# A two-layer hybrid decoder trunk: the first gate/up group computed as seven products like the rest, softmax divisors gathered, all root-mean-square sums as high/low pairs

## The chip, the cores and the metric

The kernel runs on one core of one Trainium2 chip. The metric is the device time of one execution in microseconds (us); the figure for a kernel is the median of its runs. A core has five engines with a queue of instructions each: TensorE (PE, matrix products, with a queue of its own for loading weights, PEld), VectorE (DVE), ScalarE (ACT), GpSimd (POOL) and SyncE (SP), which issues most of the transfers. An engine waits for another by semaphores.

## The reference

The input is 1024 tokens of 1024 numbers, the depth is two layers, and everything is float32. A layer normalises, projects, runs four token mixers side by side, projects back, and then runs a gated feed-forward network (FFN) of inner width 2816:

```python
for l in range(DEPTH):
    h = rmsnorm(x, attn_norm[l])
    proj = h @ w_in[l]
    (c_q, c_kv, k_r, g_b, g_c, u_conv, u_pool,
     q_sw, k_sw, v_sw) = jnp.split(proj, pts, axis=-1)
    y_a = mla_attention(c_q, c_kv, k_r, ...)      # causal softmax, 4 heads
    y_b = short_gated_conv(g_b, g_c, u_conv, conv_w[l])
    y_c = multiscale_pool(u_pool, pool_w[l], pool_scale[l])
    y_d = swa_sink_attention(q_sw, k_sw, v_sw, ...)   # window 128, a sink logit per head
    gf = jnp.stack([y_a, y_b, y_c, y_d], axis=2).astype(jnp.float32)
    gf = gf * lax.rsqrt(jnp.mean(gf * gf, axis=-1, keepdims=True) + RMS_EPS)
    mixed = gf.reshape(b, s, D_MIX) * mix_norm[l]
    x = x + mixed @ w_o[l]
    h2 = rmsnorm(x, ffn_norm[l])
    gate, up = jnp.split(h2 @ w_gate_up[l], 2, axis=-1)
    x = x + (jax.nn.silu(gate) * up) @ w_down[l]
return rmsnorm(x, final_norm)
```

## The kernel before

**Products.** Activations lie transposed: 128 channels on the partitions, tokens along the row, in two halves of 512 tokens (t = 0 and 1; `HALVES = (1, 0)`, so half 1 goes first at the end of the mixers). A float32 operand of a large product is split into a high and a low part in a reduced format (fp32r): ACT casts the high part, DVE subtracts it from the original (`split`, L368 and L371; with a gain column L373 and L374). `mm3` (L348) then makes three matmuls for each term of a product: high by high, high by low, low by high.

**Gate and up.** The FFN's 2816 gate and 2816 up columns are taken in 22 groups f of 128 gate and 128 up columns. A group over both token halves is a 2 x 2 block product (even and odd channel blocks by two halves), and a Strassen-like scheme makes it from seven products instead of eight. A product is 4 channel pairs by three matmuls, so 12 matmuls of 128 x 128 by 128 x 512. Its operands on the activation side are `hb[B11]`, `hb[B21]` (half 1 alone), `hb[B22]` (half 0, odd blocks) and the sums N1, N2, T3, T4 of both halves, which `combine(j)` (L1229) makes for pair j: two scalings on ACT, five operations on DVE, and four splits. On the weight side it needs three sums of weight blocks, which POOL makes for most groups (`GateUp.sums`).

**The first groups of a layer.** Group 0 is done plainly (`plain(u)`, L1509): four products for each half, with B11 and B21 for half 1, and B12 and B22 for half 0. No sums stand ahead of it. Groups 1 and 2 are "early": their weight sums are made in DRAM during the mixers by accumulating transfers from POOL's queue (`gu_made`, L322, six transfers a group, each held back by `paced` until a matmul of the current projection), and their steps `start`, `n2`, `n1`, `t3`, `b22`, `t4` are written out by hand around `plain` and `combine`. Group 3 and the later ones run in a loop with their sums on POOL.

**Entry of the FFN.** `out_last(t, ma)` (L1259) adds the last part of the output projection for half t (eight products of six matmuls), and for each block d DVE adds it to the residual (L1274), splits the block by the norm's gain (L374), and adds its square to the sum (L420). So half 1 gives B11 and B21; half 0 gives B12 and B22; `combine(j)` needs both.

**Roots.** The root mean square of each token is a sum over partitions, made by a matmul with a matrix of ones (`SumSq.rnorm`). If the sum's object is a pair (`SumSq(n, True)`), the sum is split into high and low and takes two fp32r matmuls (L428); else it takes one float32 matmul (L431). ACT then makes ln, exp and a square, DVE two more operations (L440, L443).

**Softmax.** In the windowed attention `swa_unit(g, i)` does one key/value group and one block of 128 queries for two heads: scores, maximum, exp with its sum, the sink's exp, addition, reciprocal (L721), scaling of the probabilities (L723), transposes and the product with the values. In the latent attention `scores(h, t, q)` does four query blocks; for each it adds the sums of its two key chunks (t = 1 alone, L1102), takes the reciprocal (L1103) and scales (L1107 on ACT, L1109 on DVE). `mix_values` of one step is called after `scores` of the next.

**Order.** A planner in the kernel (class `Order`) takes the traced instructions, gives each a cost by its kind, lists them engine by engine by due times, tries changes, and fixes the order on every engine, the PSUM banks and the places in SBUF. So a change of the program moves instructions everywhere.

Of the kernel before, what the change touches and what calls it, by code (L numbers as in the profile page):

```python
# [20 lines left out]
P = 128  # L21
# [22 lines left out]
NSP = 3  # L44
NG = NFF // 2
# [81 lines left out]
def trunk_kernel(ctx: ExitStack, tc: tile.TileContext, ins, out, given=None, ends=None):  # L127
# [13 lines left out]
    def rd(ap):  # L141
# [19 lines left out]
        {f: dpool.tile([P, 4 * HT], F32, name=f"gd{l}_{f}") for f in (1, 2)} for l in range(L)  # L161
# [296 lines left out]
    ss = SumSq(D)  # L458
# [59 lines left out]
    for l in range(L):  # L518
# [155 lines left out]
        def swa_unit(g, i):  # L674
# [17 lines left out]
            nm, rs = small(2), small(2)  # L692
# [23 lines left out]
            es = small(2)  # L716
            sk = par[:, l * PC_N + PC_SINK + 2 * g : l * PC_N + PC_SINK + 2 * g + 2]
            dve.tensor_tensor(out=es, in0=nm, in1=sk, op=ALU.add)
            act.activation(es, es, AF.Exp)
            dve.tensor_tensor(out=rs, in0=rs, in1=es, op=ALU.add)  # L720
            dve.reciprocal(rs, rs)  # L721
            for h in range(2):
# [47 lines left out]
        units = deque((g, i) for g in range(2) for i in range(NK))  # L770

        def swa_some(n):
            for _ in range(n):
                if units and qs[2 * units[0][0]][1] is not None:
                    g, i = units.popleft()
                    swa_unit(g, i)
                    if i == NK - 1:
# [7 lines left out]
        def group_scale(g):  # L785

            sg = SumSq(2 * P, g in ("b", "bcd")[l])
# [127 lines left out]
        sq_q = SumSq(2 * P, l > 0)  # L915
# [131 lines left out]
        def scores(h, t, q):  # L1047
# [3 lines left out]
            diag = ((own[0], 0), (own[1], 0), (own[0], P), (own[2], 0))  # L1051
            for b in range(4):
# [9 lines left out]
                rs = small(2)  # L1062
# [38 lines left out]
                if nch == 2:  # L1101
                    dve.tensor_tensor(out=rs[:, 0:1], in0=rs[:, 0:1], in1=rs[:, 1:2], op=ALU.add)  # L1102
                dve.reciprocal(rs[:, 0:1], rs[:, 0:1])  # L1103
                for c in range(nch):
                    a = chunks[c]
                    if c < t and b % 2:
                        act.activation(a, a, AF.Copy, scale=rs[:, 0:1])  # L1107
                        continue
                    dve.tensor_scalar(  # L1109
                        out=a, in0=a, scalar1=rs[:, 0:1], scalar2=None, op0=ALU.mult  # L1110
                    )
                pr.append(chunks)
# [146 lines left out]
        def out_last(t, ma):  # L1259
# [4 lines left out]
            for d in range(NK):  # L1264
# [11 lines left out]
                hb[c][d // 2] = half_split(a, pcol(l, PC_FFN + d))  # L1276
# [11 lines left out]
        class GateUp:  # L1288
# [20 lines left out]

            def split_plain(self):  # L1310
                self.s1, self.s2 = pair_split(self.raw[0]), pair_split(self.raw[1])
                for i in self.raw:
                    F.free_pair(i)
# [34 lines left out]
            def start(self):  # L1348
# [7 lines left out]
                mul_to(self.gate, self.gate, r2[0])  # L1356

            def n2(self):
# [3 lines left out]
                self.own.append(F.half())  # L1362
                self.gate1 = F.ap(self.own[1])
# [16 lines left out]
            def b22(self):  # L1380
                onto(self.pc, tuple(R.ap(i) for i in self.s4), hb[B22])
                for i in self.s4:
                    R.free(i)
# [1016 lines left out]
```

## Time and profile before

| what | us |
|---|---|
| median of three runs | 2031.27 (2031.17 to 2031.62) |
| the profiled execution, its own time | 2031.74 |
| its span from the first to the last instruction | 2030.0 |
| busy in the span: PE / DVE / ACT / POOL | 2018.6 / 1531.2 / 1022.6 / 567.5 |

The two layers lie one after the other: mixers of the first layer to about 360 us, its FFN to about 1015 us, then the second layer. "Busy" of PE is by the profile's modelled ends of matmuls, which overlap; how often a matmul starts says more. Views named below: the page (engine busy times and the chain that ended last), the waits (who waited for whom), the windows (busy time of each engine in a stretch, with the number of instructions in brackets), the timeline (start, length, line, operation) and the groups of instructions by line.

### The profile page before, as it was taken

Reading aid. Unit: us, or ns where it says so; the run is one execution under the profiler, and the core shown is the slowest. Engines: PE = TensorE matmul, PEld = TensorE weight load, DVE = VectorE, ACT = ScalarE, POOL = GpSimd, SP = SyncE. Lnnn points to the kernel's source line nnn. Section 1 sums busy time; section 2 is a strip of 40 time slices with the busy share of each in tenths; the row PEclk is TensorE's granted clock in tenths of the full one; section 3 lists DMA queues with packets and bytes.
Section 4 is the critical chain, followed back from the end, with each engine's and each line's share of the span. In section 5 each row is a group of like instructions: output and inputs, shape, how many; then the busy total and the mean of one; then the engine's idle time right before and its main releaser. Section 6 shows DMA issues by size and latency. Waiting matters only on the chain.

```text
span 2030.0 us, 26831 instructions
## 1 busy us (share of the span) xinstructions
PE 2018.6 (99%) x9418; PEld 1676.7 (83%) x9418; DVE 1531.2 (75%) x2442; ACT 1022.6 (50%) x1778; POOL 567.5 (28%) x428
## 2 busy tenths in 40 slices
PE   9999999999999999999999999999999999999998
PEld 7888888888888888888888888888888888888887
DVE  8779989997666678776646998799976766785554
ACT  7447657843333335555633676677333333354343
POOL 0100000057776772000001000000587677710000
PEclk9999999999999999999999999999999999999999
DMA  5431132336445547998835224332554554487552
GB/s 207 109 63 55 64 108 81 136 131 205 169 164 201 175 163 266 354 371 283 296 100 133 63 91 133 105 126 93 175 168 169 199 172 169 162 301 259 190 178 84
DMA packets 154232, 338.57 MB, mean 167 GB/s; under 512 B 14960, under 2 KB 62192, under 8 KB 154096
## 3 DMA queue, kind: packets, MB, share of 16 engines
q1 hardware_dynamic: 149616, 325.31, 46.6%
q0 software_dynamic: 4480, 11.54, 3.2%
q8 instruction: 74, 1.21, 0.2%
q14 instruction: 62, 0.51, 0.1%
HBM read 241.36 MB, written 105.91 MB: 171 GB/s over the span
## 4 chain that ended last, share of the span: by engine, by line
PE 96%; DVE 0%; DMA 0%; ACT 0%; issue 0%; DVEq 0%; ACTq 0%
PE ps_mm L348 37%; PE ps_s L348 30%; PE ps_t L348 12%; PE ps_pv L348 8%; PE ps_pv L1137 2%; PE ps_t L1125 1%; PE ps_s L1071 1%; PE ps_s L1072 1%; PE ps_s L1073 1%; PE ps_s L685 1%; PE ps_s L943 1%; PE ps_pv L746 1%; PE ps_t L734 1%; PE ps_t L428 0%; DMA xp<-u 0%; PE ps_t L431 0%
## 5 line engine op out<-in xcount | busy, mean ns | idle before, releaser
L348 PE MATMUL ps_mm<-u,u 128*128 128x512 f32 (+1 forms) x3378 | 833.2, 390 | 0.5 <-ACT u L368 0.3
L348 PEld LDWEIGHTS ps_mm<-u,u 128*128 128x128 f32 x3378 | 614.6, 188 | 122.7 <-issue 2.6
L371 DVE TENSOR_TENSOR u<-u,u 128x1024 fp32r<-128x1024 f32 (+3 forms) x453 | 511.3, 1148 | 194.1 <-ACT u L368 176.5
L348 PE MATMUL ps_s<-u,u 128*128 128x512 f32 x2670 | 634.0, 389 | 0.0
L348 PEld LDWEIGHTS ps_s<-u,u 128*128 128x128 f32 x2670 | 501.0, 188 | 104.9 <-issue 0.5
L368 ACT CAST u<-u 128x1024 fp32r<-128x1024 f32 (+3 forms) x453 | 385.2, 868 | 382.9 <-DMA u<-ad 73.9
L348 PE MATMUL ps_t<-u,u 128*128 128x512 f32 (+1 forms) x1124 | 254.4, 377 | 0.0
L348 PEld LDWEIGHTS ps_t<-u,u 128*128 128x128 f32 x1124 | 202.7, 188 | 39.3 <-issue 0.5
L1548 POOL TENSOR_TENSOR tm<-tm,u 128x512 f32<-128x512 f32 x80 | 139.5, 1744 | 341.6 <-ACT tm L1546 337.1
L348 PE MATMUL ps_pv<-u,u 128*128 128x512 f32 x744 | 177.5, 389 | 0.0
L348 PEld LDWEIGHTS ps_pv<-u,u 128*128 128x128 f32 x744 | 139.5, 188 | 29.1 <-ACT u L1364 0.2
L322 POOL DMA_DIRECT2D gd<-in_w_gu x24 | 21.6, 898 | 415.0 <-PE ps_t L348 281.4
L1134 POOL MEMSET u<- 128x128 f32 x32 | 6.1, 217 | 428.7 <-PE ps_mm L348 193.5
L1546 ACT ACTIVATE tm<-tm 128x512 f32<-128x512 f32 x80 | 50.6, 632 | 135.8 <-DVE tm L449 135.7
L368 ACT CAST u<-ps_t 128x512 fp32r<-128x512 f32 (+3 forms) x132 | 65.8, 504 | 54.1 <-PE ps_t L1125 27.0
L371 DVE TENSOR_TENSOR u<-ps_t,u 128x512 fp32r<-128x512 f32 (+3 forms) x132 | 75.7, 582 | 18.9 <-ACT u L368 17.2
L1414 ACT COPY tm<-ps_s 128x512 f32<-128x512 f32 x61 | 35.8, 587 | 101.7 <-PE ps_s L348 101.6
L1626 POOL TENSOR_TENSOR u<-u,u 128x352 f32<-128x352 f32 x64 | 81.4, 1272 | 1.4
L412 ACT ACTIVATE tm<-u 128x512 f32<-128x512 f32 (+1 forms) x91 | 53.9, 600 | 49.2 <-DVE u L1817 41.2
L373 ACT ACTIVATE u<-u,par 128x512 fp32r<-128x512 f32 x99 | 69.4, 715 | 17.8 <-DVE u L1274 7.6
L1626 POOL TENSOR_TENSOR u<-u 128x352 f32<-128x352 f32 x64 | 75.4, 1180 | 3.0 <-DMA u<-in_w_dn 2.8
L374 DVE SCALAR_TENSOR_TENSOR u<-u,par,u 128x512 fp32r<-128x512 f32 x99 | 72.5, 745 | 4.4 <-ACT u L373 4.1
(206 smaller groups left out, 2316.3 us busy)
## 6 DMA issues: line engine op xcount, KB each, us to landing
u<-in_w_gu SPq DMA_DIRECT2D x84, 512.0 KB, 4.1
ad<-u SPq DMA_DIRECT2D x154, 256.0 KB, 3.2
u<-ad SPq DMA_DIRECT2D x70, 512.0 KB, 5.9
u<-in_w_dn SPq DMA_DIRECT2D x64, 352.0 KB, 3.4
qd<-u SPq DMA_DIRECT2D x64, 352.0 KB, 2.5
u<-in_w_in SPq DMA_DIRECT2D x43, 512.0 KB, 5.8
u<-qd SPq DMA_DIRECT2D x32, 512.0 KB, 5.4
u<-in_w_dn SPq DMA_DIRECT2D x24, 512.0 KB, 5.4
```

The costliest lines, as they stand in the source:

```text
L322: paced(pool.dma_start(d, a, **more))
L348: last_mm = pe.matmul(o, w, r, start=start and k == 0 and i == 0, stop=stop and k == n - 1 and i == 2, skip_group_check=again,)
L368: a = act.copy(hi, f)
L371: dve.tensor_tensor(out=lo, in0=f, in1=rd(hi), op=ALU.subtract)
L373: a = act.activation(hi, f, AF.Copy, scale=gain)
L374: dve.scalar_tensor_tensor(out=lo, in0=f, scalar=gain, in1=rd(hi), op0=ALU.mult, op1=ALU.subtract)
L412: act.activation(q, f, AF.Square)
L1137: pe.matmul(py[:, c0:], v_of(j, h), R.ap(s)[:, c0:], start=j == 0 and n == 0, stop=j == nj - 1 and n == 1,)
L1414: act.copy(o, p)
L1546: last_silu = act.activation(g, g, AF.Silu)
L1548: pool.tensor_tensor(out=g, in0=g, in1=r, op=ALU.mult)
L1626: pool.tensor_tensor(out=o, in0=a, in1=b, op=ALU.add)
```

## The change

Four things in words, and the parts of the diff:

1. Group 0 becomes an early group like 1 and 2 (`EARLY = (0, 1, 2)`); `plain`, `plain_gates`, `plain_acts`, `split_plain` and B12 go. Its weight sums are made in DRAM too: six more accumulating transfers in each layer.
2. The hand-written order of the early groups is another: `start` of all three, then `split4` and `b22` of each beside `combine(2)` and `combine(3)`, then `n2` of all, then `n1`, `t3`, `t4` group by group.
3. `swa_pair` takes two query blocks together, and `scores` gathers the sums of four blocks, so additions, reciprocals and the sink's exp are done once for two or four blocks on wider tiles.
4. All `SumSq` objects that take whole halves are pairs: the first norm of the kernel, the group norms c and d and the query norm of layer 0 (two roots each, eight in all).

```diff
+EARLY = (0, 1, 2)
...
-        {f: dpool.tile([P, 4 * HT], F32, name=f"gd{l}_{f}") for f in (1, 2)} for l in range(L)
+        {f: dpool.tile([P, 4 * HT], F32, name=f"gd{l}_{f}") for f in EARLY} for l in range(L)
...
-    ss = SumSq(D)
+    ss = SumSq(D, True)
...
-            sg = SumSq(2 * P, g in ("b", "bcd")[l])
+            sg = SumSq(2 * P, True)
...
-        sq_q = SumSq(2 * P, l > 0)
+        sq_q = SumSq(2 * P, True)
...
+        def swa_pair(g, i):
+
+            nm, rs, es = small(4), small(4), small(4)
+            ps_ = [swa_scores(g, i + n, nm[:, 2 * n :], rs[:, 2 * n :]) for n in range(2)]
...
             act.activation(es, es, AF.Exp)
             dve.tensor_tensor(out=rs, in0=rs, in1=es, op=ALU.add)
             dve.reciprocal(rs, rs)
+            for n in range(2):
+                swa_values(g, i + n, ps_[n], rs[:, 2 * n :])
...
-                if nch == 2:
-                    dve.tensor_tensor(out=rs[:, 0:1], in0=rs[:, 0:1], in1=rs[:, 1:2], op=ALU.add)
-                dve.reciprocal(rs[:, 0:1], rs[:, 0:1])
...
+            both = sums8.rearrange("p (b c) -> p b c", c=2)
+            inv = small(4)
+            if t:
+                dve.tensor_tensor(out=inv, in0=both[:, :, 0], in1=both[:, :, 1], op=ALU.add)
+                dve.reciprocal(inv, inv)
+            else:
+                dve.reciprocal(inv, both[:, :, 0])
+            for b, chunks in enumerate(pr):
+                for c, a in enumerate(chunks):
...
-                hb[c][d // 2] = half_split(a, pcol(l, PC_FFN + d))
+                if c != B12:
+                    hb[c][d // 2] = half_split(a, pcol(l, PC_FFN + d))
...
                 dve.tensor_tensor(out=self.gate, in0=pd, in1=k1, op=ALU.add)
-                mul_to(self.gate, self.gate, r2[0])
+
+            def b22(self):
+                p = ps("ac")
+                product(p, tuple(R.ap(i) for i in self.s4), hb[B22])
...
+                self.gate1 = F.ap(self.own[1])
+                act.copy(self.gate1, p)
 
             def n2(self):
                 onto(self.pa, blocks(self.s2, 1), hb[N2])
...
+                dve.tensor_tensor(out=self.gate1, in0=self.pa, in1=self.gate1, op=ALU.add)
+                mul_to(self.gate, self.gate, r2[0])
                 silu(self.gate, r2[0])
...
-        plain(0)
-        r2.append(F.ap(ss2.rnorm(HALVES[0], tag="pv")))
-        plain_gates()
-        combine(0)
+        r2.append(F.ap(ss2.rnorm(HALVES[0], tag="t")))
         for w in early:
             w.split2()
         early[0].start()
+        r2.append(F.ap(ss2.rnorm(HALVES[1], tag="t")))
+        combine(0)
+        early[1].start()
         combine(1)
-        r2.append(F.ap(ss2.rnorm(HALVES[1], tag="t")))
-        plain_acts()
-        plain(1)
-        early[1].start()
-        combine(2)
...
+        early[2].start()
+        for j, w in zip((2, 3, None), early):
+            if j:
+                combine(j)
+            w.split4()
+            w.b22()
         for w in early:
             w.n2()
...
```

What the planner makes of it, at two places.

On PE in the mixers of layer 0, the root of the pool mixer's norm. `ps_t` is the root's bank, `ones_r` the matrix of ones, the other rows are a projection. Before:

```order
L348 MATMUL ps_mm_1541<-u24_247,u36_1309 128x512 x2
L348 MATMUL ps_mm_1541<-u24_247,u22_1310 128x512
L348 MATMUL ps_mm_1566<-u27_299,u36_1309 128x512 x2
L431 MATMUL ps_t_1415<-u16_1410,ones_r_99 128x512
L348 MATMUL ps_mm_1566<-u27_299,u22_1310 128x512
L348 MATMUL ps_mm_1566<-u29_310,u36_1309 128x512 x2
```

Now:

```order
L349 MATMUL ps_mm_1514<-u21_222,u22_1286 128x512 x2
L349 MATMUL ps_mm_1514<-u21_222,u38_1287 128x512
L349 MATMUL ps_mm_1514<-u23_237,u22_1286 128x512 x2
L429 MATMUL ps_t_1388<-u4_1385,ones_r_101 128x512 x2
L349 MATMUL ps_mm_1514<-u23_237,u38_1287 128x512
L349 MATMUL ps_mm_1514<-u24_249,u22_1286 128x512 x2
```

One float32 matmul has become two fp32r matmuls. Over the program eight go and sixteen come.

On PE at the entry of the FFN of layer 0, where the first matmuls with N2 stand (N2 of pair 0 is `u47_2205` and `u15_2217` as operand of `ps_s_4157` before, `u15_2184` and `u2_2196` as operand of `ps_s_4008`, `ps_s_4066` and `ps_pv_4114` now). Before:

```order
L348 MATMUL ps_s_4220<-u24_4059,u7_3918 128x512 x2
L348 MATMUL ps_s_4220<-u24_4059,u13_3919 128x512
L348 MATMUL ps_s_4157<-u47_2205,u20_4149 128x512
L348 MATMUL ps_s_4157<-u15_2217,u20_4149 128x512
L348 MATMUL ps_s_4157<-u47_2205,u0_4150 128x512
L348 MATMUL ps_t_4219<-u47_2205,u7_3918 128x512
L348 MATMUL ps_t_4219<-u15_2217,u7_3918 128x512
L348 MATMUL ps_t_4219<-u47_2205,u13_3919 128x512
L348 MATMUL ps_t_4219<-u16_3984,u7_3918 128x512 x2
```

Now:

```order
L349 MATMUL ps_t_4115<-u1_3806,u31_4004 128x512 x2
L349 MATMUL ps_s_4008<-u15_2184,u42_3996 128x512
L349 MATMUL ps_s_4008<-u2_2196,u42_3996 128x512
L349 MATMUL ps_s_4008<-u15_2184,u44_3997 128x512
L349 MATMUL ps_s_4066<-u15_2184,u13_4000 128x512
L349 MATMUL ps_t_4115<-u1_3806,u23_4005 128x512
L349 MATMUL ps_t_4115<-u17_3836,u31_4004 128x512 x2
L349 MATMUL ps_t_4115<-u17_3836,u23_4005 128x512
L349 MATMUL ps_s_4066<-u2_2196,u13_4000 128x512
L349 MATMUL ps_s_4066<-u15_2184,u24_4001 128x512
L349 MATMUL ps_pv_4114<-u15_2184,u31_4004 128x512
```

Before, the plain products of half 0 (`ps_s_4220`, `ps_t_4219`) stood around the first N2 matmuls. They are gone; now the three groups take N2 pair by pair in turn, between the last matmuls of the third group's `start` (`ps_t_4115`). From the first residual addition of `out_last` to the last split of N2, DVE's queue holds 88 instructions before and 70 now (60, 25 and 3 of them, and now 51, 18 and 1, are of 512 elements, of 512 elements with a gain column, and of 1024 elements). From the matmul after the first product of `out_last` to the first one that needs that last split PE's queue holds 259 matmuls before and 193 now. In layer 1 the same stretch, taken from the root ahead of it, has 80 on DVE (56, 21 and 3) and 229 on PE now.

More of the change, by code (lines that the diff above doesn't have):

```diff
@@ L1378, in t3 @@
                 dve.tensor_tensor(out=self.up, in0=self.pa, in1=self.up, op=ALU.add)
[L1380 to L1383, printed above, removed]
-                dve.tensor_tensor(out=self.gate1, in0=self.pc, in1=self.gate1, op=ALU.add)
-                mul_to(self.gate1, self.gate1, r2[1])
             def t4(self):
@@ L1494, in trunk_kernel @@
             ring_drop()
-        std = GateUp(0)
-        std.split_plain()
-        early = [GateUp(f, made[l]) for f in (1, 2)]
+        early = [GateUp(f, made[l]) for f in EARLY]
         for w in early:
@@ L1503, in trunk_kernel @@
                 R.free_pair(i)
[L1506 to L1536 removed]
+        acts = {}
+        pending = None
+        r2 = []
         def neg_mul(o, a, b):
```

106 lines of the change are left out of this document (39 added, 67 removed).

## The prediction

> **What bounds the kernel now.** I read the page's busy times first, then the chain that ended last, then PE's waits.
>
> ```profile
> span 2030.0 us, 26831 instructions
> PE 2018.6 (99%) x9418; PEld 1676.7 (83%) x9418; DVE 1531.2 (75%) x2442; ACT 1022.6 (50%) x1778; POOL 567.5 (28%) x428
> ...
> PEclk9999999999999999999999999999999999999999
> ...
> PE 96%; DVE 0%; DMA 0%; ACT 0%; issue 0%; DVEq 0%; ACTq 0%
> ```
>
> The chain is PE for 96% of the span and the clock is full in every slice. A modelled "busy" could still hide gaps, so I asked PE's waits and the start-to-start time of matmuls:
>
> ```profile
> PE ps_pv L579 <- DVE ones_r L198: 1.3, 1, 1.3
> PE ps_s L435 <- ACT tm L434: 0.5, 1, 0.5
> PE ps_mm L348 <- ACT u L368: 0.3, 1, 0.3
> ...
> 477.18 5.44 PE ps_s L348 x24
> ```
>
> All waits are the start (1.3), the last root (0.5) and a few of 0.2 to 0.3 us. In the chain, 24 matmuls of 512 columns take 5.44 us: 0.2267 us each, and this is PE's price of a matmul. So time falls only by what is taken from PE, and rises only where PE is made to wait. Where is PE nearest to waiting? The windows of the FFN's entry in layer 0, with those of layer 1 behind:
>
> ```profile
> core 0: us, PE busy (x) PEld busy (x) DVE busy (x) ACT busy (x) POOL busy (x), PEclk, DMA share, GB/s
> 360.00:380.00 20.00, 20.00 (x90) 16.55 (x89) 19.90 (x31) 14.10 (x23) 0.00 (x0) 1.00 0.51 181
> 380.00:400.00 20.00, 20.00 (x90) 16.54 (x89) 20.00 (x33) 18.04 (x31) 0.00 (x0) 1.00 0.21 80
> 1360.00:1380.00 20.00, 20.00 (x90) 16.58 (x89) 19.43 (x31) 13.21 (x21) 0.00 (x0) 1.00 0.52 184
> 1380.00:1400.00 20.00, 20.00 (x90) 16.48 (x89) 20.00 (x34) 18.71 (x32) 0.00 (x0) 1.00 0.28 106
> ```
>
> There DVE has no pause (20.00 of 20 us) while PE is full too: two engines level, and the change takes work from both.
>
> **The change part by part.**
>
> *Group 0 with seven products.* Eight products of 12 matmuls become seven: 12 fewer in each layer, 24 in all, which is the chain's row: 24 x 0.2267 = 5.4 us off PE. PE never waits there now, so it counts in full if the entry keeps PE fed (below).
>
> *Roots as pairs.* Eight float32 matmuls go, sixteen fp32r ones come. What does a float32 one hold PE for? The timeline around one:
>
> ```profile
> 143.35 1.78 PE L348 MATMUL ps_mm<-u,u 128*128 128x512 f32 x7
> 144.97 1.02 PE L431 MATMUL ps_t<-u,ones_r 128*128 128x512 f32 x2
> 145.43 1.96 PE L348 MATMUL ps_mm<-u,u 128*128 128x512 f32 x6
> 147.23 0.64 PE L685 MATMUL ps_s<-u,u 128*128 128x256 f32 x4
> ```
>
> It stands as two records, 0.46 us to the next start. But the six matmuls behind it take 147.23 - 145.43 = 1.80 us where six at 0.2267 take 1.36: another 0.44 us is its own. So 0.90 us, against 2 x 0.2267 = 0.45 for a pair. Bounds: with 0.46 alone nothing is gained, with 0.90 it is 8 x 0.45 = 3.6 us. I take 3.6, since the lost 0.44 us stands behind this matmul and not behind others of the same stretch. The Trainium skill ("FP8 and Floating Point Precision", section "TensorE Precision Notes") says that true FP32 takes four passes through the array; by that rule it would be 4 x 0.2267 = 0.91 us and the gain 3.7 us, and the trace agrees with 0.90.
>
> The pair costs a split: one cast on ACT and one subtraction on DVE, about 0.6 us each, ahead of the root.
>
> ```profile
> L368 ACT CAST u<-u 128x512 fp32r<-128x512 f32 x117 | 72.3, 619 | 104.5 <-DVE u L891 28.5 <-POOL u L1336 19.6 <-POOL u L1626 14.1
> ```
>
> In the mixers PE waits for no root (the list above), and the root's result is late by these 1.2 us less what PE saves; I cost it at nothing. If that cover went, 8 x 1.2 = 10 us could show at most, against which the whole waits of PE after the start, under 2 us, speak.
>
> *Softmax gathered.* These rows are what is thinned out:
>
> ```profile
> L1103 DVE RECIPROCAL sm<-sm 128x1 f32<-128x1 f32 x64 | 9.4, 156 | 1.1 <-ACT u L1093 0.6
> L721 DVE RECIPROCAL sm<-sm 128x2 f32<-128x2 f32 x32 | 5.1, 160 | 0.5
> L1102 DVE TENSOR_TENSOR sm<-sm 128x1 f32<-128x1 f32 x32 | 4.7, 153 | 1.9 <-ACT u L1093 1.1 <-ACT u L1090 0.8
> ```
>
> L1103 goes from 64 to 16, L1102 from 32 to 8, and L721 with its two additions from 96 to 48: 120 operations of about 0.155 us, 19 us of DVE, and 16 small exps on ACT. All lies in the mixers, where PE does not wait for them, so it earns nothing. It costs something only where a first block now waits for the last one of its group (a rival below).
>
> *POOL's transfers.* Six more in each layer, in the queue ahead of the memsets that the latent attention's values need. The last transfer and the first memset of layer 0:
>
> ```profile
> 110.47 1.13 POOL L322 DMA_DIRECT2D gd<-in_w_gu  x1 [6.92 <-DMA gd<-in_w_gu]
> 118.29 0.85 POOL L322 DMA_DIRECT2D gd<-in_w_gu  x1 [6.69 <-DMA gd<-in_w_gu]
> 217.74 0.35 POOL L1134 MEMSET u<- 128x128 f32 x2 [98.61 <-PE ps_mm L348]
> ```
>
> One every 8 us or so (118.29 - 110.47): six take some 47 us, and the queue stands idle for 98 us before the memset. Nothing.
>
> *The entry of the FFN.* This is the term against the gain. N2 needs the residuals of both halves. Before that PE can do what needs one half: before, the plain products (96 matmuls) and two `start`s (48), 144 in all; now three `start`s (72) and three `b22` (36), 108. So 36 matmuls of cover go, 8.2 us in each layer. DVE too has less to do (no splits of B12, no gates of group 0, later weight splits). What is left? DVE's prices there, start to start, and both ends of the stretch in layer 0:
>
> ```profile
> 384.42 0.74 DVE L374 SCALAR_TENSOR_TENSOR u<-u,par,u 128x512 fp32r<-128x512 f32 x1
> 385.08 0.68 DVE L420 TENSOR_TENSOR u<-u,tm 128x512 f32<-128x512 f32 x1
> 385.68 0.68 DVE L1274 TENSOR_TENSOR u<-u,ps_s 128x512 f32<-128x512 f32 x1
> ...
> 396.86 1.21 DVE L371 TENSOR_TENSOR u<-u,u 128x1024 fp32r<-128x1024 f32 x1
> 398.00 0.68 DVE L449 TENSOR_TENSOR tm<-ps_mm,u 128x512 f32<-128x512 f32 x1
> ```
>
> ```profile
> 360.45 0.84 PE L348 MATMUL ps_t<-u,u 128*128 128x512 f32 x3
> ...
> 418.76 1.52 PE L348 MATMUL ps_s<-u,u 128*128 128x512 f32 x6
> ```
>
> ```profile
> 360.65 0.69 DVE L1274 TENSOR_TENSOR u<-u,ps_s 128x512 f32<-128x512 f32 x1
> ...
> 402.87 0.69 DVE L1355 TENSOR_TENSOR u<-ps_t,tm 128x512 f32<-128x512 f32 x1 [0.93 <-PE ps_t L348]
> ...
> 417.82 0.68 DVE L371 TENSOR_TENSOR u<-tm,u 128x512 fp32r<-128x512 f32 x1
> ```
>
> So an operation of 512 costs 0.60 us, with a gain column 0.66, one of 1024 1.14. Before, from the first residual addition to the last split of N2: 60 x 0.60 + 25 x 0.66 + 3 x 1.14 = 55.9 us on DVE, and on PE up to the matmul that needs it 259 x 0.2267 = 58.7: a margin of 2.8. In truth that split ended at 417.82 + 0.68 = 418.50 and its matmul, third of the row at 418.76, started at 419.2: 0.7 us. The sum is 2.1 us too kind; 0.9 of it is a pause of DVE for PE (402.87). Now: 51 x 0.60 + 18 x 0.66 + 1.14 = 43.6 on DVE and 193 x 0.2267 = 43.8 on PE: a margin of 0.2, less those 2.1 or, without the pause, 1.2: PE is 1.0 to 1.9 us short. In layer 1 from the root ahead: 56 x 0.60 + 21 x 0.66 + 3 x 1.14 = 50.9 against 229 x 0.2267 = 51.9, a margin of 1.0, of which the root's way over ACT to DVE takes about 2 (three casts' worth of 0.62): some 1 to 2 us short again. I take 1.5 us a layer, 3.0 in all. Bounds: nothing, if DVE's pauses fill, and the whole lost cover, 2 x 8.2 = 16.3 us, if DVE's smaller load were of no use. Behind N2 the operands of N1, T3 and T4 come with more time, because 108 matmuls of them follow.
>
> *The "row factor".* The diff has no new multiplication: `mul_to` of the gate moves from `start` to `n2`. Nothing.
>
> **Sum.** Span 2030.0 - 5.4 - 3.6 + 3.0 = 2024.0 us. The profiled execution took 2031.74, 1.74 around its span, and the median of three runs lies 1.27 above that span: 2024.0 + 1.27 = 2025.3 us.
>
> **The rivals.**
>
> *No price at the entry* (2022.3). The planner places matmuls by when their operands come, and DVE's own pause shows play. Against it: DVE at 20.00 of 20 us.
>
> *Half of the lost cover shows* (8.2 us instead of 3.0): 2030.5, no change to be told. For it: ACT at 18.04 of 20 us beside DVE, so casts and subtractions wait for each other; against it: ACT loses four scaled casts of B12 here too.
>
> *The pairs earn nothing* (0.46 us is all that a float32 matmul holds PE): 2025.3 + 3.6 = 2028.9, no change either. Against it: the 1.80 us above.
>
> *The entry starves PE* (slower). If all 16.3 us show, 2031.27 - 9.0 + 16.3 = 2038.6; it is slower than before from 9.0 us on, and measurably from 13. Its place is N2 to T4 of the early groups: three groups side by side hold more banks and slots than two, so DVE's results of one must leave before the next may start. For it: both queues are full today. Against it: 18 fewer operations on DVE ahead of N2. The Trainium skill ("TensorE: Matmul & The Clock Gate", section "What's actually happening") adds that after an idle window of about 3.4 us PE's clock falls to half until it has been busy as long; by that rule a hole longer than this would cost about 1.7 us more (an estimate from that page). No run here shows it: the granted clock is full and the longest wait 1.3 us.
>
> *Gathering holds up the mixers.* The first block's transposes wait for the scores of three more blocks, at most 3 x 6 x 0.2267 = 4.1 us in a step of half 1. `mix_values` runs a step behind `scores`, so it shows at most at the last step, 4.1 us a layer: 2033.5, no change.
>
> **How the numbers follow.** This kernel's change can be told from none at about 0.2%, 4.1 us: faster is below 2027.2, slower above 2035.3. Forecast (1 to 4 us lost at the entry) 0.59; no price 0.16; half of the cover 0.10; pairs without gain 0.03; mixers held up 0.05; starved entry 0.07. So faster 0.75, the same 0.18, slower 0.07. The forecast's own range is 2023 to 2027. For 8 in 10 I go from 2021.0 (no price, and a little from the thinner mixers) to 2031.0 (half of the cover): above lie the starved entry and a part of the held-up mixers.
>
> **What would show it.** Right: PE's records fall from 9418 to 9394 (24 fewer; a float32 matmul stands as two records, so the roots change nothing); no float32 root of 512 columns is left; 24 fewer L348 matmuls of 512 columns; PE's waits list splits or casts (DVE or ACT) at the entries, 1 to 2 us in each of the layers, in several pieces below 1 us; DVE still at 20 of 20 us there and POOL's transfers done before the memsets. Wrong: waits of PE in the mixers on L1129 or on the pair's split; a stretch of slow PE with a lower granted clock; or two waits of several us at N2. If the time is about 2022, the entry cost nothing; if it is above 2030, the cover was worth more than the sum of the queues says.

## The result and the profile after

The changed kernel takes 2034.47 us (median of 21 runs, 2033.77 to 2035.44) against 2031.62 us of the kernel before (21 runs, 2030.82 to 2032.88): a ratio of 1.0013, with a 95% interval of 1.0007 to 1.0019. That is 2.9 us slower. The interval leaves out 1, but the difference lies within the 0.2% that the prediction calls no change. The forecast was 6 us faster, and its range ended at 2031.0. The profiled execution's span is 2032.4 us, 2.4 more than before.

The page of the changed kernel, its busy times and its chain:

```profile
span 2032.4 us, 26706 instructions
PE 2016.4 (99%) x9394; PEld 1670.0 (82%) x9394; DVE 1543.8 (76%) x2338; ACT 1026.1 (50%) x1772; POOL 575.8 (28%) x440
...
PE 89%; DVE 5%; ACT 2%; DMA 1%; issue 1%; DVEq 0%; ACTq 0%
```

PE has the 24 records less that were forecast and is "busy" for 2.2 us less, but the chain that ended last runs through PE for only 89% of the span (96% before); 9% of it is now DVE, ACT and others for which PE waits. Its five longest waits:

```profile
PE ps_t L429 <- DVE tm L441: 1.4, 3, 0.7
PE ps_t L349 <- DVE u L372: 1.4, 2, 1.0
PE ps_pv L580 <- DVE ones_r L199: 1.3, 1, 1.3
PE ps_t L752 <- DVE tm L741: 0.7, 1, 0.7
PE ps_s L436 <- ACT tm L435: 0.5, 1, 0.5
```

The third and the fifth row were there before. L429 is the root's matmul, L441 the DVE operation that reads the root's bank, L372 a split. The entries of both layers by windows (engine busy time, and in brackets the instructions that start):

```profile
core 0: us, PE busy (x) PEld busy (x) DVE busy (x) ACT busy (x) POOL busy (x), PEclk, DMA share, GB/s
380.00:400.00 20.00, 19.33 (x82) 14.77 (x81) 20.00 (x33) 18.38 (x32) 0.00 (x0) 1.00 0.26 93
...
1380.00:1400.00 20.00, 19.53 (x84) 15.16 (x82) 20.00 (x33) 17.69 (x30) 0.00 (x0) 1.00 0.31 118
1400.00:1420.00 20.00, 18.90 (x82) 15.12 (x82) 19.90 (x32) 13.13 (x23) 0.00 (x0) 1.00 0.25 67
```

Before, the last of these windows was:

```profile
1400.00:1420.00 20.00, 20.00 (x90) 16.57 (x89) 19.03 (x30) 13.29 (x22) 1.42 (x1) 1.00 0.17 53
```

DVE is full, as before, but PE starts 82 and 84 matmuls in 20 us where it started 90. At 0.2267 us each the eight that are missing in the first row are 1.8 us, while the busy column lacks only 0.67. A modelled matmul lasts 0.39 us and the next starts after 0.2267, so a gap shorter than about 0.16 us does not appear as idle time, and a longer one appears 0.16 us too short.

So I made an account of my own from the starts. For each matmul I took the time to the next start, and called its usual value (the median over both kernels for the same kind of matmul with the same neighbours) PE's own work, and what is above it waiting. It was made for every run below; each line is one trace, and the two kernels seven_alone and seven_sums_on_pool, whose matmuls are the same, differ by 0.4 us in it, so less than that is not read. "Own" is against the 2012.7 us of before; "mixers" are 30 to 357 and 1010 to 1357 us, "entries" 357 to 430 and 1357 to 1430 us. The level of the waiting hangs on how finely the kinds are drawn: with kinds by shape alone all waiting is 9.3 us before and 20.8 in the changed kernel, while the difference, 11.5, stays. So only differences are read. The traced executions of seven_alone and changed_long_search took 1.4 and 1.3 us more than the medians of their kernels.

| kernel | median us | own | mixers, layer 0 / 1 | entries, layer 0 / 1 | all waiting |
|---|---|---|---|---|---|
| before | 2031.4 to 2031.7 | 0 | 3.5 / 3.9 | 0.0 / 0.2 | 7.0 |
| changed | 2034.47 | -9.2 | 6.4 / 6.8 | 2.4 / 3.2 | 18.6 |
| pairs_alone | 2035.93 | -3.2 | 7.6 / 4.6 | 1.2 / 0.8 | 14.2 |
| gather_alone | 2031.38 | -0.6 | 3.4 / 2.9 | 0.9 / 0.5 | 7.0 |
| seven_alone | 2037.06 | -5.4 | 5.2 / 4.1 | 2.6 / 7.7 | 19.0 |
| changed_without_pairs | 2036.37 | -6.0 | 5.2 / 6.5 | 1.9 / 4.2 | 17.7 |
| changed_draw2 | 2034.60 | -9.2 | 5.8 / 6.4 | 2.2 / 4.1 | 18.5 |
| before_draw2 | 2032.03 | 0 | 3.7 / 3.6 | 0.0 / 0.2 | 6.8 |
| changed_long_search | 2035.38 | -9.1 | 7.1 / 7.7 | 1.9 / 4.3 | 21.0 |
| changed_sums_on_pool | 2030.24 | -9.2 | 5.5 / 5.8 | 1.8 / 0.7 | 14.5 |
| without_pairs_sums_on_pool | 2032.43 | -6.0 | 5.9 / 6.3 | 0.9 / 0.7 | 13.8 |
| seven_sums_on_pool | 2033.16 | -5.8 | 5.2 / 6.0 | 1.3 / 1.2 | 14.4 |
| before_sums_on_pool | 2034.09 | +0.1 | 3.8 / 4.1 | 0.2 / 2.1 | 9.5 |
| changed_sums_on_pool_long | 2031.20 | -9.2 | 5.8 / 6.2 | 1.7 / 0.6 | 15.3 |
| split_load_alone | 2031.33 | 0 | 3.2 / 3.1 | -0.1 / 0.1 | 6.6 |
| late_alone | 2032.24 | 0 | 4.2 / 4.8 | 0.1 / 0.2 | 8.2 |
| first_norm_pair | 2031.53 | -0.9 | 2.8 / 3.7 | 1.3 / 0.2 | 7.3 |
| mixer_pairs | 2035.34 | -2.6 | 6.2 / 5.2 | 1.2 / 0.8 | 12.9 |
| query_pair | 2032.53 | -1.0 | 3.4 / 4.2 | 1.1 / 0.2 | 8.9 |
| changed_pool_query_f32 | 2033.65 | -8.3 | 7.2 / 6.0 | 3.1 / 0.7 | 17.0 |

For the changed kernel: -9.2 + (18.6 - 7.0) = 2.4 us, the difference of the spans. PE's own work fell as forecast. PE waits 11.6 us more: 5.4 at the entries, 5.8 in the mixers, 0.4 elsewhere. So the gain was made in full and more than given back.

What a wait at the entry looks like: layer 1, PE and then DVE (start, length, line; in square brackets the idle time before and what ended it).

```profile
1398.12 0.73 PE L349 MATMUL ps_t<-u,u 128*128 128x512 f32 x2
1399.32 0.73 PE L429 MATMUL ps_t<-u,ones_r 128*128 128x512 f32 x2 [0.47 <-DVE tm L441]
1401.05 4.31 PE L349 MATMUL ps_t<-u,u 128*128 128x512 f32 x16 [1.00 <-DVE u L372]
```

```profile
1397.38 0.68 DVE L1376 TENSOR_TENSOR u<-ps_t,tm 128x512 f32<-128x512 f32 x1
1397.98 0.68 DVE L372 TENSOR_TENSOR u<-u,u 128x512 fp32r<-128x512 f32 x1
1398.58 0.68 DVE L441 SCALAR_TENSOR_TENSOR tm<-ps_t,tm 128x512 f32<-128x512 f32 x1
1399.18 1.81 DVE L372 TENSOR_TENSOR u<-u,u 128x512 fp32r<-128x512 f32 x2
```

The second half's root doesn't use the first half's result; it starts at 1399.32, just after DVE has read the first half's root from its bank (L441, ended at 1399.26), so it waits for that bank. The next matmul needs the low part of the second early group's weights. This split is the second of the two L372 that end at 1400.99 (by its length of about 1.2 us it is the one of 1024 elements), and the first is that of an operand of T3, which no matmul takes for some 100 more; PE starts at 1401.05. Neither wait is for N2's operand: DVE has no pause, and what PE needs from it stands a place or two too far back.

### The profile page after: what moved, and what is told of

Same layout as the page of the kernel before. It is cut to its first block, busy times and chain, and to the rows that moved or that the text cites. A ratio compares the mean times of both kernels' runs of the same rounds, so it can differ in the third digit from the quotient of the medians.

```text
span 2032.4 us, 26706 instructions
## 1 busy us (share of the span) xinstructions
PE 2016.4 (99%) x9394; PEld 1670.0 (82%) x9394; DVE 1543.8 (76%) x2338; ACT 1026.1 (50%) x1772; POOL 575.8 (28%) x440
## 4 chain that ended last, share of the span: by engine, by line
PE 89%; DVE 5%; ACT 2%; DMA 1%; issue 1%; DVEq 0%; ACTq 0%
PE ps_mm L349 34%; PE ps_s L349 27%; PE ps_t L349 10%; PE ps_pv L349 8%; PE ps_pv L1162 2%; PE ps_t L1150 2%; DVE u L372 1%; PE ps_s L1092 1%; PE ps_s L1094 1%; PE ps_s L1093 1%; PE ps_s L686 1%; PE ps_pv L764 1%; DVE u L375 1%; PE ps_t L752 1%; DVE u L421 1%
## 5 line engine op out<-in xcount | busy, mean ns | idle before, releaser
L372 DVE TENSOR_TENSOR u<-u,u 128x1024 fp32r<-128x1024 f32 (+2 forms) x465 | 523.6, 1149 | 158.9 <-ACT u L369 136.8
L369 ACT CAST u<-u 128x1024 fp32r<-128x1024 f32 (+3 forms) x465 | 392.3, 864 | 375.8 <-DMA u<-ad 71.3
L349 PEld LDWEIGHTS ps_s<-u,u 128*128 128x128 f32 x2628 | 493.1, 188 | 103.4 <-ACT u L374 0.4
L349 PE MATMUL ps_pv<-u,u 128*128 128x512 f32 x792 | 191.9, 389 | 0.0
L349 PEld LDWEIGHTS ps_pv<-u,u 128*128 128x128 f32 x792 | 148.4, 188 | 31.1 <-ACT u L369 0.2
L323 POOL DMA_DIRECT2D gd<-in_w_gu x36 | 32.1, 891 | 487.2 <-PE ps_t L349 292.4
L372 DVE TENSOR_TENSOR u<-ps_t,u 128x512 fp32r<-128x512 f32 (+3 forms) x132 | 74.7, 581 | 17.8 <-ACT u L369 17.2
L1357 POOL TENSOR_TENSOR u<-u 128x512 f32<-128x512 f32 x38 | 68.4, 1801 | 38.1 <-DVE u L372 38.1
L450 DVE TENSOR_TENSOR tm<-tm,u 128x512 f32<-128x512 f32 x76 | 74.1, 976 | 2.1
```

Of the source, the lines that this page charges most:

```text
L349: last_mm = pe.matmul(o, w, r, start=start and k == 0 and i == 0, stop=stop and k == n - 1 and i == 2, skip_group_check=again,)
L369: a = act.copy(hi, f)
L372: dve.tensor_tensor(out=lo, in0=f, in1=rd(hi), op=ALU.subtract)
L450: dve.tensor_tensor(out=o, in0=a, in1=b, op=ALU.mult)
L1357: pool.tensor_tensor(out=q4, in0=q4, in1=F.ap(self.raw[1] + 1), op=ALU.add)
```

## The experiments

**The parts one by one.** Into the kernel before I put one part of the change at a time, and I took the pairs out of the changed kernel.

pairs_alone:

```diff
-    ss = SumSq(D)
+    ss = SumSq(D, True)
-            sg = SumSq(2 * P, g in ("b", "bcd")[l])
+            sg = SumSq(2 * P, True)
-        sq_q = SumSq(2 * P, l > 0)
+        sq_q = SumSq(2 * P, True)
```

> The kernel before with the eight float32 roots as pairs and nothing else. PE's own work should fall by 8 x 0.45 = 3.6 us. Theory A (the pair's split, on DVE and ACT ahead of the root, is what makes PE wait in the mixers): 3.6 less some 6 us of waits, so 1 to 3 us above the kernel before. Theory B (the gathered softmax makes the mixers' waits): 3 to 4 us below before. Theory C (the waits are how the planner's order happened to fall): anything within 2 us of 3.6 below.

gather_alone has part 3 of the change (`swa_pair` and the gathered `scores`), seven_alone has parts 1 and 2 (`EARLY = (0, 1, 2)`, the new order of the early groups):

> The kernel before with the windowed softmax in pairs of blocks and the latent softmax with its divisors gathered, and nothing else. PE's own work stays. Theory A: within 1 us of before. Theory B (a first block waits for the last of its group, and PE with it): 4 to 6 us above before, with PE's waits on L1129's successors or on the transposes. Theory C: within 2 us either way.

> The kernel before with group 0 as an early group of seven products and nothing else. PE's own work should fall by 24 x 0.2267 = 5.4 us. If the waits at the two entries of the FFN, 5.4 us more in the changed kernel than before, come from the lost cover alone, it ends within 1 us of before, with the waits between 380 and 420 us and between 1380 and 1420 us. If the entry's waits need the other edits too, it ends 3 to 5 us below before.

changed_without_pairs is the changed kernel with the three lines of pairs_alone turned back:

> The changed kernel with the eight roots as float32 again. PE's own work rises by 3.2 to 3.6 us against the changed kernel. If the pairs cost what they cost alone (7 us of waits, mostly in the mixers), it ends 3 to 4 us below the changed kernel, near 2031. If their waits in the changed kernel are covered by what gathering freed on DVE, it ends at or above the changed kernel's 2034.5.

Measured: pairs alone 2035.93 us, ratio 1.0022 (1.0013 to 1.0032); gathering alone 2031.38, 1.0000 (0.9990 to 1.0009); seven products alone 2037.06, 1.0027 (1.0015 to 1.0038); without the pairs 2036.37, 1.0023 (1.0014 to 1.0032). Gathering earns and costs nothing, as forecast. Each of the other two makes the kernel before slower, by some 4.3 and 5.4 us, though PE's own work falls nearly as the prediction said (3.2 of 3.6 us and 5.4 of 5.4). Both lie above every case that was expected of them. The parts do not add: 4.3 + 5.4 - 0.3 = 9.4 us alone, 2.9 together, and within the changed kernel the pairs are worth 1.9 us (2036.37 - 2034.47). PE's waits of seven_alone:

```profile
PE ps_t L349 <- DVE u L1352: 3.3, 2, 2.6
PE ps_pv L580 <- DVE ones_r L199: 1.3, 1, 1.3
PE ps_t L349 <- DVE u L372: 1.1, 2, 0.8
```

L1352 is the addition that ends a `start` and frees the bank of its second product. Again DVE holds PE at the entry. In the account the entries wait for 10.1 us more than before, which is more than seven products save. (1.4 us of this are a slower clock in the traced execution; see the last section.)

**Is it the draw of the planner?** The same programs with another seed (`random.Random(2)`), and the planner with 300 tries instead of 30.

> The changed kernel, with another seed for the planner's random tries, so the same work in another order. Theory C: 2 us or more away from the changed kernel's 2034.5, most likely below. Theories A and B: within 1 us of it.

> The kernel before with another seed of the planner (630 lines of difference in PE's order). If the order of before is a lucky draw, which any change of the program loses, this takes 2033 to 2036. If the draw is worth little, 2031 to 2032, as the changed kernel's second draw was worth 0.1 us.

> The changed kernel, the planner trying 300 instead of 30 improvements of its order. If the new waits are what a short search leaves, the time falls by 2 to 5 us, to 2030 to 2032. If they are in the program's own dependencies and loads, it stays at 2033.5 to 2035.5. Another seed of the same length gave 2034.60.

> The changed kernel with the FFN norm's plain additions on POOL (2030.24 us) and 300 tries of the planner. If a longer search also removes waits in the mixers, 2026 to 2029, below before; if not, 2029 to 2031.

Measured: 2034.60 us for the second draw of the changed kernel (ratio to before 1.0014, 1.0005 to 1.0024), 2032.03 of the kernel before (1.0002, 0.9992 to 1.0012); 2035.38 with the long search (1.0018, 1.0008 to 1.0027), and 2031.20 with the long search and the edit below (0.9998, 0.9989 to 1.0008). One other seed each moves the time by 0.1 and 0.5 us, and ten times the search made both kernels, if anything, 1 us slower. So there is no sign that the order of before was a lucky draw, and a longer search of this kind doesn't remove the waits. Whether a planner with other costs would was not tried.

**Is it DVE's load at the entry?** The 24 plain additions of the FFN norm's sums of squares go from DVE to POOL, which is idle there: in the changed kernel, without its pairs, with seven products alone, and in the kernel before as the control.

```diff
-        def __init__(self, n, pair=False):
+        def __init__(self, n, pair=False, on=dve):
...
-                dve.tensor_tensor(out=a, in0=a, in1=q, op=ALU.add)
+                self.on.tensor_tensor(out=a, in0=a, in1=q, op=ALU.add)
...
-        ss2 = SumSq(D, True)
+        ss2 = SumSq(D, True, pool)
```

> The changed kernel with the 12 plain additions of the FFN norm's sum of squares in each layer on POOL, which stands idle there, instead of DVE: 7 us less of DVE at each entry. If DVE's load is what makes PE wait at the entries, the 5.6 us of waits there fall below 1.5 and the time falls by 4 to 5 us, below the kernel before. If the waits come from a bank or an operand that is late whatever DVE's load, or if POOL's additions are late or block DVE, the time stays or rises.

> Both of the above: seven products and gathering, float32 roots, the FFN norm's additions on POOL. If both causes are right and add up, some 7 us below the changed kernel, at 2027 to 2028: 5.4 us of PE's work saved, and few waits more than before. If they do not add, between 2030 and 2034.

> Before with group 0 as seven products alone (2037.06 us, waits of PE 12 us above those of before, 10 of them around the two entries), and the plain additions of the FFN norm's sum of squares moved from DVE to POOL. Theory: DVE's queue is the one that PE waits for at the entry, so its relief takes most of these 10 us: 2028 to 2031. Rival: the order of the hand-written groups or the banks hold PE there, and DVE's load is not what decides without the other two edits: 2034 to 2037.

> The kernel before with the plain additions of the FFN norm's sum of squares on POOL. PE's waits at its entries are only 0.2 us, so if the relief is worth something only where the cover is short, this takes 2031 to 2032. If it helps elsewhere too, it is 2028 to 2030, and the 4 us that the same edit gave the changed kernel are not the entry's.

Measured: 2030.24 us (0.9996, 0.9986 to 1.0005), 2032.43 (1.0005, 0.9995 to 1.0014), 2033.16 (1.0005, 0.9996 to 1.0015) and 2034.09 (1.0015, 1.0006 to 1.0024). The edit takes 4.2, 3.9 and 3.9 us from the three kernels with seven products and adds 2.6 to the one without. In the account the entries' waits fall from 5.6 to 2.5, from 6.1 to 1.6 and from 10.3 to 2.5 us, and rise from 0.2 to 2.3 in the control. The windows of changed_sums_on_pool, against those of the changed kernel above:

```profile
1380.00:1400.00 20.00, 19.79 (x88) 16.05 (x87) 20.00 (x27) 18.28 (x32) 6.61 (x5) 1.00 0.25 90
1400.00:1420.00 20.00, 20.00 (x90) 16.54 (x89) 19.91 (x32) 11.41 (x19) 0.00 (x0) 1.00 0.28 80
```

In the first of these windows six operations fewer start on DVE, and PE starts 88 and 90 matmuls instead of 84 and 82. The waits fall less far than expected (2.5 us left, not 1.5), without_pairs_sums_on_pool shows that taking out the pairs and relieving DVE don't add, seven_sums_on_pool lies between the two cases named for it, and the control lies above both of its cases. The traces show why the relief is small. 24 additions at 0.60 us from start to start are 14.4 us off DVE's queue. But while POOL adds, DVE operations that read two operands from SBUF can take longer. The split with a gain column in the kernel before and then in before_sums_on_pool (the three durations are the least, the median and the most, in ns):

```profile
L374 DVE SCALAR_TENSOR_TENSOR u<-u,par,u x99: 732/744/753, 6.4 to 1397.4; 128x512 fp32r<-128x512 f32 x99
```

```profile
L374 DVE SCALAR_TENSOR_TENSOR u<-u,par,u x99: 726/746/1877, 6.7 to 1402.8; 128x512 fp32r<-128x512 f32 x99
```

The residual additions (L1274), which read one operand from PSUM, keep their 0.67 to 0.69 us beside POOL. Taken against the median of the same operation while POOL adds nothing, DVE's operations beside the moved additions are 16.6 us longer in the control and 10.4, 10.3 and 9.1 us in the other three. So the edit takes a net 4.0 to 5.3 us from DVE in the three kernels with seven products, and their time falls by about as much; in the control it adds 2.2 us to DVE, PE's waits at the entries rise by 2.1 us, and the time by 2.6. All four go the way of DVE's load, so DVE's load is what PE waits for at the entry. What a real relief would do with the old cover the control doesn't tell. The operation on POOL, in before_sums_on_pool:

```profile
L420 POOL TENSOR_TENSOR u<-u,tm x24: 1293/1626/2272, 368.2 to 1398.2; 128x512 f32<-128x512 f32 x24
```

Its median of 1.63 us stands against 0.68 for the same addition on DVE. Whether a later root costs something too is not shown. Of the 7.8 us that the trace of seven_alone wins at the entries 3.9 show in the medians: 1.9 us of waits came back in the mixers of layer 1 and 1.3 elsewhere, for which I have no cause, and the traced execution of seven_alone was one of its slower ones.

changed_sums_on_pool is the best version that was run, 1.1 us below the 2031.38 of before on the same chip, which can't be told from no change.

**Why do the pairs cost so much alone?** They save 3.2 us of own work and bring 7.2 us of waits. Two candidates: the splits' load on ACT and DVE, and the root's lateness behind its split. split_load_alone makes the eight splits in the kernel before and uses none; late_alone also makes the float32 root wait for the subtraction.

```diff
                 if cols == whole and self.pair:
                     self.hl[t] = half_split(a)
+                elif cols == whole:
+                    for h in half_split(a):
+                        R.free(h)
...
-                pe.matmul(p, ones, a, start=True, stop=final is None)
+                m = pe.matmul(p, ones, a, start=True, stop=final is None)
+                if t in self.late:
+                    d = self.late.pop(t)
+                    tc.add_manual_dep(m.ins, d.ins.name, ..., reason="late")
```

> The kernel before with the casts and subtractions of the eight pairs made as in the pairs but used by nothing; the roots stay float32 matmuls that wait for no split. If the load on DVE and ACT is the cost of a pair, PE waits about 7 us more as in the run with pairs alone: 2036 to 2039. If it is the root's lateness behind the split, the time stays within 1 us of before.

> The kernel before with its float32 roots, the eight pairs' casts and subtractions made (their results unused), and each float32 root's matmul made to wait for the subtraction of its own half, as the pair's matmuls do. The splits without that wait took 2031.33 us, the pairs 2035.93. If what the pairs cost is that the root comes later behind its split, the waits of PE rise by some 7 us as with the pairs, and since a float32 root is 0.40 us dearer than a pair, the time is 2036 to 2039. If the cost is only where the planner happens to put things in the pairs' program, it is 2031 to 2033.

Measured: 2031.33 us (0.9998, 0.9989 to 1.0008) and 2032.24 us (1.0004, 0.9994 to 1.0013). Neither is the price, and late_alone lies in the range that was named for where the planner happens to put things. Load and lateness together bring 1.2 us of the 7.2. The starts in pairs_alone agree: just ahead of the roots' matmuls in the mixers PE loses 0.8 us, and 0.2 in the kernel before. Then I divided the pairs by place: the first norm's two, the six of the mixers, the query norm's two alone, and the changed kernel (with the sums on POOL) with the query norm's back in float32.

> Of the eight pairs only the two of the program's first norm; the other six roots stay float32. All eight together took 2035.93 us with 7 us of new waits. One of the longest of these waits (0.9 to 1.3 us) is at 59 us, before any root of the mixers but after the first norm's, so if the order that the planner makes behind the first norm is what costs, most of the loss is here: 2033 to 2035. If the mixers' roots cost it, two roots give 0.8 us and cost nothing: 2030.5 to 2031.5.

> The other six pairs alone (group norms c and d and the query norm of layer 0), the first norm float32. If the mixers' roots cost it, 2033 to 2036; if the first norm's, six roots give 2.4 us: 2029 to 2030.5. If both parts come out near 2034, each redraw of the order costs, whatever its place.

> Of the eight pairs only the two of layer 0's query norm. With six pairs in the mixers the time was 2035.34 us, with 6 us of new waits, 0.9 of them at 229 us right behind this norm's root, where DVE is nearly full. If this norm's lateness is what costs, this takes 2033 to 2035. If it is spread over the three norms, each two roots cost about 1.3 us net: 2032 to 2033. If the group norms cost it, 0.8 us are gained: 2030.5 to 2031.5.

> The changed kernel with the FFN norm's plain additions on POOL (2030.24 us), and layer 0's query norm back to float32 roots. PE's own work rises by 0.8 us. If the query norm's pair brings waits of 2 us or more, 2027.5 to 2029.5; if it brings none, 2030.5 to 2031.5.

Measured: 2031.53 us (1.0001, 0.9991 to 1.0010), 2035.34 (1.0019, 1.0009 to 1.0028), 2032.53 (1.0004, 0.9995 to 1.0014) and 2033.65 (1.0013, 1.0004 to 1.0021). The first norm's pair costs nothing; the mixers' six cost 3.9 us net, with 5.9 us of waits, 2.7 of them in the mixers of layer 0 where they stand. The longest there, in mixer_pairs, PE and then DVE:

```profile
226.73 0.40 PE L428 MATMUL ps_t<-u,ones_r 128*128 128x512 f32 x1
226.96 1.09 PE L348 MATMUL ps_mm<-u,u 128*128 128x512 f32 x4
228.76 1.42 PE L348 MATMUL ps_mm<-u,u 128*128 128x512 f32 x5 [0.71 <-DVE tm L449]
```

```profile
226.76 0.68 DVE L449 TENSOR_TENSOR u<-u,u 128x512 f32<-128x512 f32 x1
227.36 0.74 DVE L374 SCALAR_TENSOR_TENSOR u<-u,par,u 128x512 fp32r<-128x512 f32 x1
228.03 0.68 DVE L449 TENSOR_TENSOR tm<-ps_mm,u 128x512 f32<-128x512 f32 x1
```

PE waits for DVE to empty a projection's bank (L449, ended at 228.71), not for a root. Nor is this one of the changed roots. The root in front of it is that of group norm b, which is a pair in the kernel before too, where this row stands at the same place:

```profile
228.61 0.40 PE L428 MATMUL ps_t<-u,ones_r 128*128 128x512 f32 x1
```

The expectation of query_pair takes it for the query norm's; the roots that query_pair turns into pairs stand at 180 and 186 us in the kernel before. So that run says nothing of this wait. The query norm costs 1.0 us alone, and turning it back in the changed kernel made that one 3.4 us slower, outside both cases that were expected, where its own work adds 0.8. So the query norm isn't the cause by itself. The group norms c and d were not run alone; by subtraction they cost 3 us net, but the parts don't add. What stays open is how six pairs in the mixers turn 2.6 us of saved work into 5.9 us of waits. Left are the group norms, the two places in SBUF that a pair holds until its root, which I didn't try, and the many moves that the planner makes for each of these edits.

## Why the prediction was wrong, point by point

**PE is the bound, and its own work falls by 5.4 + 3.6 us.** Right: 9.2 us by the account. Seven products gave 5.4 (24 x 0.2267); the pairs 3.2, so 0.40 us a root where 0.45 was worked out from 0.90 against 0.45; gathering has the other 0.6, little above the 0.4 that isn't read. The rival that pairs earn nothing on PE falls with it. The 3.7 us that the Trainium skill's four passes would give ("FP8 and Floating Point Precision", section "TensorE Precision Notes") are 0.5 above the account too.

**Gathering 0, POOL's transfers 0.** Right. gather_alone is at before's time. POOL's queue in the changed kernel:

```profile
160.32 0.85 POOL L323 DMA_DIRECT2D gd<-in_w_gu  x1 [6.94 <-DVE u L375]
215.98 0.35 POOL L1159 MEMSET u<- 128x128 f32 x2 [54.80 <-PE ps_mm L349]
```

The last transfer is issued at 160 us, 42 us later than before, and the memset still waits 54.80 us for PE alone.

**The entry costs 3.0 us.** The engine was right, the place and the size were not: 5.4 us. This term was the margin at N2, DVE's sum against PE's. It took DVE as one heap of work whose last piece matters. The waits that the list names stand ahead of N2's products, at a bank that DVE has to read (L441, in seven_alone L1352) and at the weight split that stands behind one of T3 (1401.05). The moves to POOL show that DVE's load is behind them. Three `start`s and two roots now use tiles named `ps_t`, where the first root had `ps_pv` before; but the planner places all tiles in the eight banks whatever their names, and no run changed this, so that it brings the waits is not shown. The prediction named three groups holding more banks, but only in the rival that starves PE, with 16.3 us; the truth lies at a third of that.

**"In the mixers PE waits for no root [...] I cost it at nothing."** This step failed, and it is the larger part: 5.8 us. It failed twice. It took the list of waits for the whole, and the list shows no gap below about 0.16 us. In the mixers of the kernel before it names four waits of 0.2; by the starts 36 matmuls come more than 0.03 us late, 4.1 us in all. (The rest of the account's 7.4 us is in differences below 0.03 us and may be no waiting.) In the changed kernel 75 come late, 9.6 us in all. So the mixers had less cover than the list shows. That work taken from PE there brings it sooner to where DVE or ACT isn't ready is my reading; no run shows it. And of what the pairs add, the step priced load and lateness, which are indeed cheap (1.2 us), and not the moves that follow. What in those moves makes PE wait stays open. Even without the pairs the changed kernel waits 4.3 us more in the mixers than before (11.7 against 7.4), which the parts alone (+1.9 with seven products, -1.1 with gathering) don't give.

**The sum.** From 2025.3 to 2034.5 are 9.2 us: 5.8 in the mixers, 2.4 more at the entries, 0.4 elsewhere, 0.8 because the median lies 2.1 and not 1.3 us over the profiled span, less the 0.2 that the own work fell beyond the forecast. The range reached to "half of the cover", which holds for the entries; it had no case in which the mixers wait in many short pieces. The sign "waits of PE in the mixers on L1129 or on the pair's split" was looked for in the right place; the longest waits there name other lines (L741 and L441 in the changed kernel, L449 in mixer_pairs).

## What to carry to other kernels

Where an engine is full and another is level with it, count its starts and not its busy time: in the mixers late starts were 4 us before the change where the list of waits named 0.8, and a microsecond taken from the full engine was not all earned. A margin between two queues has to be taken at each bank and operand in their order, not once over the sum of a stretch. Work that is moved to an idle engine can slow the one that it leaves: of 14.4 us taken from DVE here 9 to 17 came back. And edits to a kernel with a planner don't add: two that each lost 4 to 5 us lost 3 together, so a part is judged within the whole as well as alone.

## What was not expected of the hardware

**The clock can fall after short holes.** In the traced execution of seven_alone PE started no matmul between 1399.96 and 1403.09 us, the 2.6 us of idle time in its waits above, and two microseconds later its granted clock was halved for 3.4 us (by the four windows below full clock). The windows of 1 us; the granted clock is the third number from the right:

```profile
1401.00:1402.00 1.00, 0.00 (x0) 0.00 (x0) 1.00 (x3) 0.76 (x2) 0.00 (x0) 1.00 0.00 0
1402.00:1403.00 1.00, 0.00 (x0) 0.00 (x0) 1.00 (x3) 1.00 (x2) 0.00 (x0) 1.00 0.00 0
1403.00:1404.00 1.00, 0.73 (x2) 0.30 (x2) 1.00 (x2) 0.90 (x3) 0.00 (x0) 1.00 0.00 0
1404.00:1405.00 1.00, 0.78 (x3) 0.67 (x4) 1.00 (x3) 0.97 (x2) 0.00 (x0) 1.00 0.00 0
1405.00:1406.00 1.00, 1.00 (x4) 0.78 (x3) 1.00 (x3) 0.67 (x2) 0.00 (x0) 0.57 0.39 27
1406.00:1407.00 1.00, 1.00 (x3) 0.74 (x3) 1.00 (x2) 0.36 (x2) 0.00 (x0) 0.50 0.66 211
1407.00:1408.00 1.00, 1.00 (x4) 0.77 (x3) 1.00 (x3) 0.92 (x3) 0.00 (x0) 0.50 0.07 25
1408.00:1409.00 1.00, 1.00 (x5) 0.82 (x4) 1.00 (x2) 1.00 (x2) 0.00 (x0) 0.72 0.00 0
```

From 1405.32 to 1408.31 us seven matmuls start 0.427 us apart instead of 0.2267: 1.4 us, of the 7.7 that the account puts down to this entry. changed_long_search has the same from 1403.27 to 1406.68 us, after two idle times of 1.25 and 0.40 us within 2.4 us:

```profile
1401.11 0.73 PE L429 MATMUL ps_t<-u,ones_r 128*128 128x512 f32 x2 [1.25 <-DVE tm L441]
1402.24 5.98 PE L349 MATMUL ps_t<-u,u 128*128 128x512 f32 x18 [0.40 <-DVE u L372]
```

The changed kernel's 0.47 and 1.00 us at the same place did not bring it. The Trainium skill ("TensorE: Matmul & The Clock Gate", section "What's actually happening") has the clock halved after one idle window of about 3.4 us and gives the way back as long. The 3.4 us at half clock agree. The holes here are shorter than that window, so in these two executions less than a whole idle window was enough, and the measurement decides; how much less is not shown. So this wait, 2.9 us from start to start above the usual, cost 4.3 in this execution. By the mean granted clocks it doesn't come in every execution: three of the six of seven_alone have 0.997 (2037.61 to 2038.46 us, the traced one among them) and three 0.998 (2035.69 to 2036.51 us), and 3.4 us at half clock are 0.0008 of the span.

**A float32 root stands as two records of 0.592 us**, and yet replacing it by two fp32r ones of 0.40 us gave 0.40 us a root. The groups by line, before and then with the pairs (pairs_alone); the three durations are the least, the median and the most:

```profile
L431 PE MATMUL ps_t<-u,ones_r x16: 590/592/688, 19.2 to 195.4; 128*128 128x512 f32 x16
```

```profile
L428 PE MATMUL ps_t<-u,ones_r x56: 387/397/500, 20.6 to 1403.7; 128*128 128x512 f32 x56
```
